# Fewer input buffers, more output buffers, and eleven of 64 transposes moved to VectorE in a matmul with rotary embedding

## The chip, the cores and the metric

The kernel runs on one core of a Trainium2 chip. The metric is the time of one execution in device microseconds (us), measured on the chip; lower is better. A profile is one such execution with its trace. The span in a profile is some 1.75 us shorter than the time of the same execution (168.5 against 170.29 us for the profiled run of the kernel before).

## The reference

The kernel multiplies x by a weight matrix and rotates each head of the product by position.

```python
# x: (16, 512, 768), weight: (768, 768), cos and sin: (512, 64), 12 heads of 64
y = np.matmul(x, weight).reshape(batch, seq, n_heads, head_dim)
y1, y2 = y[..., :32], y[..., 32:]
out1 = y1 * cos1 - y2 * sin1      # cos1, sin1: first halves, by position
out2 = y2 * cos2 + y1 * sin2
out = np.concatenate([out1, out2], axis=-1)
```

Inputs and outputs are fp32. The kernel multiplies in fp16 and accumulates in fp32.

## The kernel before

The 8,192 rows of x make 64 tiles of 128 rows. Two tiles are a pair, numbered n = 0 to 31. A tile is loaded (SyncE's queue), cast to fp16 (ScalarE, `xc`), transposed by six TensorE instructions into PSUM (`pt`), copied to SBUF (ScalarE, `xT`) and multiplied by the weights (12 matmuls into `psy`). VectorE multiplies a whole pair by cosine and sine at once ("rope", `tq`), GpSimd adds the two products (`ov`), and a DMA issued on ScalarE's queue stores the pair.

```python
AHEAD = 8
AHEAD_B = 4
ALONE = 3                      # the last three pairs are done tile by tile
...
def by_blocks(n, s):
    return False               # no tile goes through transpose_blocks
...
xpool = ctx.enter_context(tc.tile_pool(name="xpool", bufs=24))   # x, fp32
opool = ctx.enter_context(tc.tile_pool(name="opool", bufs=4))    # output pairs
...
def load_blocks(n):
    if n >= NP or not by_blocks(n, 1):
        return
    ...
    src = x[b].rearrange("(j a r) (q k) -> r q a j k", r=SB, a=R, q=NQ)
    dst = xss[n, 1].rearrange("p (j k) -> p j k", j=NQ)
    for q in (0, 2, 1, 3):
        eng = nc.sync if q < 2 else nc.scalar
        eng.dma_start(out=dst[ts(q, R)], in_=src[r, q])
...
def transpose_blocks(n, s):    # 32x32 blocks, as four-byte words
    ...
    nc.vector.transpose(out=..., in_=x16.pop((n, s)).bitcast(FP32))
...
for n in range(2, NP):
    while loaded < min(NP, n + AHEAD):
        load_plain(loaded)
        loaded += 1
    if n + 1 < NP and by_blocks(n + 1, 1):
        transpose_blocks(n + 1, 1)
    for s in (0, 1):
        for c in CHUNKS:
            mm(n, s, *c)
        upto("turn", 2 * n + s + 3)     # TensorE transposes and ScalarE copies
        upto("cast", 2 * n + s + 5)     # ScalarE casts
        ...
    if n >= 3:
        store(n - 3, nc.scalar)
    load_blocks(n + AHEAD_B)
    if n < NP - ALONE:
        rope_pair(n)                    # VectorE, then the add on GpSimd
```

Block loads and block transposes are thus written already, and switched off. ScalarE works through its casts, its copies and its DMA issues strictly in order. A DMA issue that has to wait holds everything after it (in the runs below a copy on ScalarE stood for 2.35 us behind a block load's issue and for 5.14 us behind a store's).

Of the kernel before, what the change touches and what calls it, by code (L numbers as in the profile page):

```python
# [12 lines left out]
MULT = mybir.AluOpType.mult  # L13
ADD = mybir.AluOpType.add
# [3 lines left out]
def kernel(  # L18
# [9 lines left out]
    nc = tc.nc  # L28
    P = nc.NUM_PARTITIONS

    B, S, H = x.shape
    NH = int(n_heads)
    D = H // NH
    HD = D // 2
# [3 lines left out]
    SB = S // P  # L38
    NP = B * SB // 2
    CHUNKS = [(t, e) for t in range(NT) for e in range(2)]  # L40
    AHEAD = 8
    AHEAD_B = 4
    ALONE = 3

# [3 lines left out]
    def where(n, s):  # L48
        return 2 * (n // SB) + s, n % SB

    def by_blocks(n, s):
        return False

    konst = ctx.enter_context(tc.tile_pool(name="konst", bufs=1))
    ident = konst.tile([P, P], FP16)
# [2 lines left out]
    csn = konst.tile([P, 2, SB, D], FP32)  # L58
    w_raw = konst.tile([P, NT, 2, H], FP32)
    w_sb = konst.tile([P, NT, 2, H], FP16)  # L60

    xpool = ctx.enter_context(tc.tile_pool(name="xpool", bufs=24))
    bpool = ctx.enter_context(tc.tile_pool(name="bpool", bufs=AHEAD_B + 1))
    cpool = ctx.enter_context(tc.tile_pool(name="cpool", bufs=6))
    tpool = ctx.enter_context(tc.tile_pool(name="tpool", bufs=9))
    rpool = ctx.enter_context(tc.tile_pool(name="rpool", bufs=3))
    opool = ctx.enter_context(tc.tile_pool(name="opool", bufs=4))
    pt_pool = ctx.enter_context(tc.tile_pool(name="pt", bufs=2, space=bass.MemoryType.PSUM))
    py_pool = ctx.enter_context(tc.tile_pool(name="py", bufs=2, space=bass.MemoryType.PSUM))
    cold_ps = pt_pool.tile([P, 512], FP32, tag="pt", name="cold_ps")  # L70
# [1 line left out]
    xss, x16, xTT, psys, tqs, ovs = {}, {}, {}, {}, {}, {}  # L72
# [7 lines left out]
    def load(n, s):  # L80
        b, r = where(n, s)
        xss[n, s] = xpool.tile([P, H], FP32, tag="xs", name="xs")
        nc.sync.dma_start(  # L83
            out=xss[n, s], in_=x[b].rearrange("(p r) h -> r p h", r=SB)[r]
        )

    def load_plain(n):
        for s in (0, 1):
            if n < NP and not by_blocks(n, s):
                load(n, s)  # L90
# [40 lines left out]
    def transpose_blocks(n, s):  # L131
        xT = tpool.tile([P, NT, P, 2], FP16, tag="xT", name="xT")
        nc.vector.transpose(
            out=xT.bitcast(FP32).rearrange("p t m e -> p (t m e)"),
            in_=x16.pop((n, s)).bitcast(FP32),
        )
        xTT[n, s] = xT.rearrange("p t m e -> p t e m")
# [5 lines left out]
    def psum(n, s):  # L143
        if n < NP - ALONE:
            if n not in psys:
                psys[n] = py_pool.tile([P, 3, 512], FP32, tag="psy", name="psy")
                if n < 2:
                    nc.tensor.matmul(  # L148
                        psys[n][:, 1], cold[:, 0:P], cold, start=True, stop=False
                    )  # L150
            cut = 512 if s == 0 else 256
            return [
                (psys[n][:, s, ds(s * 256, cut)], 0, cut, n < 2 and s == 1),
                (psys[n][:, s + 1, 0 : H - cut], cut, H, n < 2 and s == 0),
            ]
        if (n, s) not in psys:
            if (2 * (n - NP + ALONE) + s) % 3 == 1:
                psys[n, s] = [
                    pt_pool.tile([P, 512], FP32, tag="pt", name="psz") for _ in (0, 1)
                ]  # L160
            else:
                ps = py_pool.tile([P, 3, 512], FP32, tag="psy", name="psy")
                psys[n, s] = [ps[:, 0], ps[:, 1]]
        lo, hi = psys[n, s]
        return [(lo, 0, 512, False), (hi[:, 0 : H - 512], 512, H, False)]

    def mm(n, s, t, e):
        for ps, lo, hi, joined in psum(n, s):
            nc.tensor.matmul(  # L169
                ps,  # L170
                xTT[n, s][:, t, e, :],
                w_sb[:, t, e, lo:hi],
                start=((t, e) == CHUNKS[0] and not joined),
                stop=((t, e) == CHUNKS[-1] and not (joined and s == 0)),
            )

    def rope(n, c0, c1, ps):
        r = n % SB
        nh = (c1 - c0) // D
        if n not in tqs:  # L180
            tqs[n] = rpool.tile([P, 2, 2 * H], FP32, tag="tq", name="tq")
            ovs[n] = opool.tile([P, 2 * H], FP32, tag="ov", name="ov")
        nc.vector.tensor_tensor(  # L183
            out=tqs[n][:, :, c0:c1].rearrange("p j (h d) -> p j h d", d=D),
            in0=ps.rearrange("p (h d) -> p h d", d=D)
            .unsqueeze(1).broadcast_to((P, 2, nh, D)),
            in1=csn[:, :, r, :].unsqueeze(2).broadcast_to((P, 2, nh, D)),
            op=MULT,
        )

    def add(n, c0, c1, eng):
        w = c1 - c0
        tq = tqs[n][:, :, ds(c0, w)]
        eng.tensor_tensor(  # L194
            out=ovs[n][:, ds(c0, w)].rearrange("p (h t d) -> p h t d", t=2, d=HD),
            in0=tq[:, 0].rearrange("p (h t d) -> p h t d", t=2, d=HD),
            in1=tq[:, 1].rearrange("p (h t d) -> p h t d", t=2, d=HD)[:, :, ::-1, :],
            op=ADD,
        )

    def rope_pair(n):
        rope(n, 0, 2 * H, psys[n].rearrange("p b n -> p (b n)"))
        add(n, 0, 2 * H, nc.gpsimd)

    def rope_alone(n, s):
        for ps, lo, hi, _ in psum(n, s):
            rope(n, s * H + lo, s * H + hi, ps)



    def rope_last(n, s, engs):
        r = n % SB
        for (ps, lo, hi, _), eng in zip(psum(n, s), engs):
            nh = (hi - lo) // D
            q = tqs[n][:, 1, ds(s * H + lo, hi - lo)]
            ph = ps.rearrange("p (h d) -> p h d", d=D)
            for o, j in ((q.rearrange("p (h d) -> p h d", d=D), 1), (ph, 0)):
                nc.vector.tensor_tensor(  # L218
                    out=o, in0=ph, op=MULT,
                    in1=csn[:, j, r, :].unsqueeze(1).broadcast_to((P, nh, D)),  # L220
                )
            nc.vector.tensor_tensor(  # L222
                out=ovs[n][:, ds(s * H + lo, hi - lo)].rearrange(
                    "p (h t d) -> p h t d", t=2, d=HD
                ),
                in0=ps.rearrange("p (h t d) -> p h t d", t=2, d=HD),
                in1=q.rearrange("p (h t d) -> p h t d", t=2, d=HD)[:, :, ::-1, :],
                op=ADD,
            )
            store(n, eng, s * H + lo, s * H + hi)  # L230

    def store(n, eng, c0=0, c1=2 * H):
        b, r = where(n, 0)
        dst = out.rearrange("b (p r) h -> r p b h", r=SB)[r, :, b : b + 2]
        src = ovs[n].rearrange("p (b h) -> p b h", b=2)
        if c1 - c0 < 2 * H:
            s = c0 // H
            dst = dst[:, s, c0 - s * H : c1 - s * H]
            src = src[:, s, c0 - s * H : c1 - s * H]
        eng.dma_start(out=dst, in_=src)  # L240
# [15 lines left out]
    nc.sync.dma_start(out=sin_sb, in_=sin.rearrange("(p r) d -> p r d", r=SB))  # L256
    for n in range(2, AHEAD):
        load_plain(n)
# [5 lines left out]
    def upto(what, k):  # L264
        k += min(4, max(0, k - 41) // 4)
        while done[what] < min(k, 2 * NP):
            n, s = divmod(done[what], 2)
            done[what] += 1
            if what == "cast":
                cast(n, s, nc.scalar)  # L270
            elif not by_blocks(n, s):
                transpose(n, s, nc.scalar)
# [13 lines left out]
    for k, c in enumerate(CHUNKS):  # L286
# [8 lines left out]
        out=csn[:, 1, :, HD:D], in0=sin_sb[:, :, 0:HD], scalar1=-1.0  # L295
    )
    rope_pair(0)
    upto("cast", 6)
    mm(1, 0, *CHUNKS[-1])
# [4 lines left out]
    upto("turn", 6)  # L304
    upto("cast", 8)
    rope_pair(1)

    loaded = AHEAD
    for n in range(2, NP):

        while loaded < min(NP, n + AHEAD):
            load_plain(loaded)
            loaded += 1
        if n + 1 < NP and by_blocks(n + 1, 1):
            transpose_blocks(n + 1, 1)
        for s in (0, 1):
            for c in CHUNKS:
                mm(n, s, *c)
            upto("turn", 2 * n + s + 3)
            upto("cast", 2 * n + s + 5)  # L320
            if n >= NP - ALONE:
                if (n, s) != (NP - 1, 1):
                    rope_alone(n, s)
                    add(n, s * H, (s + 1) * H, nc.gpsimd)
        if n >= 3:
            store(n - 3, nc.scalar)
        load_blocks(n + AHEAD_B)
        if n < NP - ALONE:
            rope_pair(n)
    store(NP - 3, nc.scalar)  # L330
    store(NP - 2, nc.scalar)
    store(NP - 1, nc.scalar, 0, H)
    rope_last(NP - 1, 1, (nc.sync, nc.sync))


# [33 lines left out]
```

## Time and profile before

| | kernel before |
|---|---|
| time, three runs | 169.1 us median (168.88 to 169.13) |
| time of the profiled run | 170.29 us (span 168.5) |
| TensorE busy | 154.7 us, 92% |
| VectorE, ScalarE, GpSimd busy | 69%, 59%, 65% |
| largest stall of TensorE after the start | 2.50 us at 55.7 us |

The profile cuts the span into 40 slices, in which a digit is the busy share in tenths. Groups of waits give who waited, for whom, the total us, how often, and the longest. The lines are in the prediction. "Granted clock" is the share of TensorE's full clock that the chip granted in a stretch.

### The profile page before, as it was taken

Reading aid. Unit: us, or ns where it says so; the run is one execution under the profiler, and the core shown is the slowest. Engines: PE = TensorE matmul, PEld = TensorE weight load, DVE = VectorE, ACT = ScalarE, POOL = GpSimd, SP = SyncE. Lnnn points to the kernel's source line nnn. Section 1 sums busy time; section 2 is a strip of 40 time slices with the busy share of each in tenths; the row PEclk is TensorE's granted clock in tenths of the full one; section 3 lists DMA queues with packets and bytes.
Section 4 is the critical chain, followed back from the end, with each engine's and each line's share of the span. In section 5 each row is a group of like instructions: output and inputs, shape, how many; then the busy total and the mean of one; then the engine's idle time right before and its main releaser. Section 6 shows DMA issues by size and latency. Waiting matters only on the chain.

```text
span 168.5 us, 2869 instructions
## 1 busy us (share of the span) xinstructions
PE 154.7 (92%) x1170; PEld 99.1 (59%) x1170; DVE 116.0 (69%) x58; ACT 99.6 (59%) x125; POOL 109.4 (65%) x38
## 2 busy tenths in 40 slices
PE   7799999999999499999999999999999999999900
PEld 2455666666666256666666666676666766665500
DVE  0566976777777707777777777776767676789970
ACT  3523876666773356677666677787898788610000
POOL 0000597739952945749997777777876767679980
PEclk9999999999999969999999999999999999999995
DMA  4999999999999999999999997444433444458666
GB/s 168 365 399 402 398 402 402 405 411 322 416 373 412 411 417 415 411 414 414 415 420 405 397 330 292 191 187 160 157 123 153 164 187 189 187 222 339 256 251 243
DMA packets 19390, 53.18 MB, mean 316 GB/s; under 512 B 1840, under 2 KB 2224, under 8 KB 19376
## 3 DMA queue, kind: packets, MB, share of 16 engines
q1 hardware_dynamic: 10656, 28.19, 43.3%
q10 hardware_dynamic: 8720, 24.81, 37.8%
q8 instruction: 9, 0.15, 0.3%
q14 instruction: 5, 0.04, 0.1%
HBM read 27.82 MB, written 25.17 MB: 314 GB/s over the span
## 4 chain that ended last, share of the span: by engine, by line
PE 66%; DMA 17%; DVE 6%; POOL 3%; ACT 1%; issue 1%; POOLq 1%; SPq 1%; ACTq 0%; DVEq 0%
PE psy L169 55%; PE pt L126 10%; DMA xs<-in_x_dram 7%; DVE tq L183 6%; DMA out_dram<-ov 6%; DMA w_raw<-in_weight_dram 4%; POOL ov L194 3%; POOLq L364 1%; SPq L83 1%; ACT xT L76 1%; ACT xc L76 1%; ACTq L240 0%; POOLq L194 0%; DVEq L183 0%
## 5 line engine op out<-in xcount | busy, mean ns | idle before, releaser
L194 POOL TENSOR_TENSOR ov<-tq 128x1536 f32<-128x1536 f32 (+1 forms) x34 | 109.2, 3220 | 54.1 <-DVE tq L183 36.4
L169 PE MATMUL psy<-w_sb,xT 128*128 128x512 f16 (+1 forms) x744 | 132.3, 328 | 2.6 <-ACT xT L76 2.5
L183 DVE TENSOR_TENSOR tq<-psy,csn 128x3072 f32<-128x3072 f32 (+2 forms) x35 | 102.6, 2945 | 39.2 <-PE psy L169 37.8
L169 PEld LDWEIGHTS <-xT 128*128 128x128 f16 x768 | 73.2, 98 | 46.2 <-ACT xT L76 2.7
L76 ACT COPY xT<-pt 128x768 f16<-128x768 f16 x62 | 49.2, 800 | 40.0 <-PE pt L126 35.4
L76 ACT CAST xc<-xs 128x768 f16<-128x768 f32 x62 | 55.4, 901 | 8.3 <-DMA xs<-in_x_dram 8.2
L126 PEld LDWEIGHTS <-xc 128*128 128x128 f16 x384 | 26.5, 99 | 10.9 <-ACT xc L76 1.9
L126 PE MATMUL pt<-ident,xc 128*128 128x128 f16 x384 | 31.6, 220 | 1.4 <-ACT xT L76 0.5
L244 PE MATMUL cold_ps<-cold 128*128 128x512 f16 x16 | 5.6, 494 | 1.2 <-DVE cold L249 1.2
L110 DVE CAST w_sb<-w_raw 128x768 f16<-128x768 f32 x6 | 3.4, 560 | 2.1 <-DMA w_raw<-in_weight_dram 2.1
L169 PE MATMUL psz<-w_sb,xT 128*128 128x512 f16 (+1 forms) x24 | 4.2, 326 | 0.0
L78 DVE CAST xc<-xs 128x768 f16<-128x768 f32 x2 | 1.9, 948 | 3.1 <-DMA xs<-in_x_dram 3.1
L244 PEld LDWEIGHTS <-cold 128*128 128x128 f16 x16 | 1.8, 123 | 3.3 <-issue 1.9
L183 DVE TENSOR_TENSOR tq<-psz,csn 128x1024 f32<-128x1024 f32 (+1 forms) x4 | 3.6, 948 | 0.0
L78 DVE COPY xT<-pt 128x768 f16<-128x768 f16 x2 | 1.1, 558 | 1.7 <-PE pt L126 1.7
L76 ACT ACT_TABLE_LOAD x1 | 1.3, 1283 | 1.1 <-PEq L350 1.1
L222 DVE TENSOR_TENSOR ov<-psy,tq 128x512 f32<-128x512 f32 (+1 forms) x2 | 1.1, 557 | 0.1
L218 DVE TENSOR_TENSOR psy<-psy,csn 128x512 f32<-128x512 f32 (+1 forms) x2 | 1.1, 556 | 0.0
L218 DVE TENSOR_TENSOR tq<-psy,csn 128x512 f32<-128x512 f32 (+1 forms) x2 | 1.1, 554 | 0.0
L249 DVE MEMSET cold<- 128x256 uint32 x1 | 0.3, 272 | 0.9 <-PEq L350 0.9
L148 PE MATMUL psy<-cold 128*128 128x512 f16 x2 | 0.8, 379 | 0.0
L293 DVE COPY csn<-sin_sb 128x128 f32<-128x128 f32 x1 | 0.2, 226 | 0.2 <-DMA sin_sb<-in_sin_dram 0.2
(6 smaller groups left out, 0.8 us busy)
## 6 DMA issues: line engine op xcount, KB each, us to landing
xs<-in_x_dram SPq DMA_DIRECT2D x64, 384.0 KB, 8.4
out_dram<-ov ACTq DMA_DIRECT2D x31, 768.0 KB, 5.6
w_raw<-in_weight_dram SPq DMA_DIRECT2D x6, 384.0 KB, 7.4
out_dram<-ov ACTq DMA_DIRECT2D x1, 384.0 KB, 3.6
out_dram<-ov SPq DMA_DIRECT2D x1, 256.0 KB, 2.3
csn<-in_cos_dram SPq DMA_DIRECT2D x1, 128.0 KB, 7.9
sin_sb<-in_sin_dram SPq DMA_DIRECT2D x1, 128.0 KB, 6.5
out_dram<-ov SPq DMA_DIRECT2D x1, 128.0 KB, 3.4
```

The costliest lines, as they stand in the source:

```text
L76: eng.copy(out=o, in_=i_)
L78: eng.tensor_copy(out=o, in_=i_)
L83: nc.sync.dma_start(out=xss[n, s], in_=x[b].rearrange("(p r) h -> r p h", r=SB)[r])
L110: nc.vector.tensor_copy(out=w_sb[:, t, e], in_=w_raw[:, t, e])
L126: nc.tensor.transpose(pt[:, t, e, :], xc[:, t, e, :], ident)
L169: nc.tensor.matmul(ps, xTT[n, s][:, t, e, :], w_sb[:, t, e, lo:hi], start=((t, e) == CHUNKS[0] and not joined), stop=((t, e) == CHUNKS[-1] ...
L183: nc.vector.tensor_tensor(out=tqs[n][:, :, c0:c1].rearrange("p j (h d) -> p j h d", d=D), in0=ps.rearrange("p (h d) -> p h d", d=D) .unsqu ...
L194: eng.tensor_tensor(out=ovs[n][:, ds(c0, w)].rearrange("p (h t d) -> p h t d", t=2, d=HD), in0=tq[:, 0].rearrange("p (h t d) -> p h t d", ...
L218: nc.vector.tensor_tensor(out=o, in0=ph, op=MULT, in1=csn[:, j, r, :].unsqueeze(1).broadcast_to((P, nh, D)),)
L222: nc.vector.tensor_tensor(out=ovs[n][:, ds(s * H + lo, hi - lo)].rearrange("p (h t d) -> p h t d", t=2, d=HD), in0=ps.rearrange("p (h t d) ...
L244: nc.tensor.matmul(cold_ps, cold[:, 0:P], cold, start=True, stop=True)
L364: with _tile.TileContext(nc) as tc:
```

## The change

The intent is to stop the loads from running far ahead of the work (ten input buffers instead of 24), to give the stores more slack (six output buffers instead of four), to take 66 transposes off TensorE, and to shorten the end.

```diff
-    AHEAD = 8
+    AHEAD = 7
     def by_blocks(n, s):
-        return False
+        return s == 1 and n % 2 == 1 and 6 < n < NP - ALONE
-    xpool = ctx.enter_context(tc.tile_pool(name="xpool", bufs=24))
+    xpool = ctx.enter_context(tc.tile_pool(name="xpool", bufs=10))
-    opool = ctx.enter_context(tc.tile_pool(name="opool", bufs=4))
+    opool = ctx.enter_context(tc.tile_pool(name="opool", bufs=6))
-    def rope_pair(n):
-        rope(n, 0, 2 * H, psys[n].rearrange("p b n -> p (b n)"))
-        add(n, 0, 2 * H, nc.gpsimd)
+    def rope_pair(n, step=2 * H):
+        ps = psys[n].rearrange("p b n -> p (b n)")
+        for c in range(0, 2 * H, step):
+            rope(n, c, c + step, ps[:, ds(c, step)])
+            add(n, c, c + step, nc.gpsimd)
     # cut: rope_last now ropes the last 256 columns first and has GpSimd add them,
     # does the first 512 in place on VectorE, and stores the two parts on two queues
-        while loaded < min(NP, n + AHEAD):
-            load_plain(loaded)
-            loaded += 1
+        load_plain(n + AHEAD - 2)
-            rope_pair(n)
+            rope_pair(n, 2 * H if n < NP - ALONE - 1 else H)
```

More of the change, by code (lines that the diff above doesn't have):

```diff
@@ L207, in rope_alone, with rope_last @@
             rope(n, s * H + lo, s * H + hi, ps)
-    def rope_last(n, s, engs):
-        r = n % SB
-        for (ps, lo, hi, _), eng in zip(psum(n, s), engs):
-            nh = (hi - lo) // D
-            q = tqs[n][:, 1, ds(s * H + lo, hi - lo)]
-            ph = ps.rearrange("p (h d) -> p h d", d=D)
-            for o, j in ((q.rearrange("p (h d) -> p h d", d=D), 1), (ph, 0)):
-                nc.vector.tensor_tensor(
-                    out=o, in0=ph, op=MULT,
-                    in1=csn[:, j, r, :].unsqueeze(1).broadcast_to((P, nh, D)),
-                )
-            nc.vector.tensor_tensor(
-                out=ovs[n][:, ds(s * H + lo, hi - lo)].rearrange(
-                    "p (h t d) -> p h t d", t=2, d=HD
-                ),
-                in0=ps.rearrange("p (h t d) -> p h t d", t=2, d=HD),
-                in1=q.rearrange("p (h t d) -> p h t d", t=2, d=HD)[:, :, ::-1, :],
-                op=ADD,
-            )
-            store(n, eng, s * H + lo, s * H + hi)
+    def rope_last(n, s):
+        (ps, _, cut, _), (pz, _, _, _) = psum(n, s)
+        c0, c1, c2 = s * H, s * H + cut, (s + 1) * H
+        rope(n, c1, c2, pz)
+        add(n, c1, c2, nc.gpsimd)
+        nh = cut // D
+        q = tqs[n][:, 1, c0:c1]
+        ph = ps.rearrange("p (h d) -> p h d", d=D)
+        for o, j in ((q.rearrange("p (h d) -> p h d", d=D), 1), (ph, 0)):
+            nc.vector.tensor_tensor(
+                out=o, in0=ph, op=MULT,
+                in1=csn[:, j, n % SB, :].unsqueeze(1).broadcast_to((P, nh, D)),
+            )
+        nc.vector.tensor_tensor(
+            out=ovs[n][:, c0:c1].rearrange("p (h t d) -> p h t d", t=2, d=HD),
+            in0=ps.rearrange("p (h t d) -> p h t d", t=2, d=HD),
+            in1=q.rearrange("p (h t d) -> p h t d", t=2, d=HD)[:, :, ::-1, :],
+            op=ADD,
+        )
+        store(n, nc.sync, c0, c1)
+        store(n, nc.scalar, c1, c2)
     def store(n, eng, c0=0, c1=2 * H):
@@ L306 @@
     rope_pair(1)
-    loaded = AHEAD
     for n in range(2, NP):
-        while loaded < min(NP, n + AHEAD):
-            load_plain(loaded)
-            loaded += 1
+        load_plain(n + AHEAD - 2)
         if n + 1 < NP and by_blocks(n + 1, 1):
@@ L332 @@
     store(NP - 1, nc.scalar, 0, H)
-    rope_last(NP - 1, 1, (nc.sync, nc.sync))
+    rope_last(NP - 1, 1)
 _INS = ['x', 'weight', 'cos', 'sin', 'n_heads']
```

## The prediction

> **What bounds the kernel now.** I read the page's list of busy engines first, then the busy tenths, then the chain of work that ended last. TensorE is the candidate: it is busy 92% of the span and every other engine at most 69%.
>
> ```profile
> span 168.5 us, 2869 instructions
> PE 154.7 (92%) x1170; PEld 99.1 (59%) x1170; DVE 116.0 (69%) x58; ACT 99.6 (59%) x125; POOL 109.4 (65%) x38
> PE   7799999999999499999999999999999999999900
> DMA  4999999999999999999999997444433444458666
> ```
>
> A busy TensorE alone proves little, so the reader should look at the zeros, the 4 in the fifteenth slice (59 to 63 us), and the last row: the DMA engines are full until slice 24 (about 100 us) and then less than half busy. The chain says whether TensorE really sets the pace. Its columns are start, length and what ran:
>
> ```profile
> 58.25 3.40 PE psy L169 x12
> 61.65 0.64 PE pt L126 x6
> 62.29 2.04 PE psy L169 x12
> 64.33 0.34 PE pt L126 x6
> 64.67 1.95 PE psy L169 x12
> 66.62 0.33 PE pt L126 x6
> 66.95 1.95 PE psy L169 x12
> ```
>
> From 16.4 us to 37.5 us and from 58 us to 148 us it is nothing but TensorE: 12 matmuls of 1.95 us, then six transposes of 0.34 us, per tile of 128 rows: 2.285 us a tile, 4.57 us a pair. The first line is the exception. The groups of waits say why:
>
> ```profile
> DVE tq L183 <- PE psy L169: 37.8, 27, 5.6
> POOL ov L194 <- DMA out_dram<-ov: 17.7, 10, 5.1
> ACT xT L76 <- POOL ov L194: 4.6, 1, 4.6
> PE psy L169 <- ACT xT L76: 2.5, 1, 2.5
> ```
>
> Columns: total us, times, longest. Lines two to four are one sequence, and the timeline from 44 to 62 us gives its order. GpSimd's add for a pair waits 5.14 us for one of four output buffers, because that buffer's store takes 9.63 us to land; ScalarE, which issues stores in order between its copies, then sits 4.58 us on a store whose add isn't done; TensorE, needing the xT that ScalarE has not copied, idles 2.50 us at 55.7 us. The table of windows shows the aftermath (the columns here are stretch, its length, busy time of PE, PEld, DVE, ACT, POOL, then granted clock, DMA share, GB/s):
>
> ```profile
> 37.00:57.00 20.00, 18.75 (x151) 12.37 (x149) 14.91 (x5) 11.14 (x14) 13.50 (x4) 1.00 1.02 386
> 57.00:62.00 5.00, 3.75 (x18) 2.11 (x19) 1.88 (x1) 3.09 (x4) 3.74 (x2) 0.69 1.03 414
> 62.00:92.00 30.00, 30.00 (x238) 19.86 (x237) 20.29 (x7) 20.72 (x26) 21.80 (x7) 0.99 1.03 414
> ```
>
> The granted clock falls to 0.69, so 12 matmuls take 3.40 instead of 1.95 us. Whole cost: matmul groups start at 53.30 and 64.67 us, three tiles later; 11.37 us instead of 3 x 2.285 = 6.86, so **4.5 us are lost to one stall**.
>
> The end is a second regime. TensorE stops at 159.96 us (timeline), the profile at 168.5. There GpSimd is the last link: its adds run back to back from 151.47 to 163.77 us (one of 3.46, five of about 1.77), and the store of the last one closes the span.
>
> **What the Trainium skill says.** "VectorE: DVE Perf Modes", The three transpose paths: VectorE transposes only within blocks of 32x32, and puts 128x128 bf16 at 311 ns. That is why the change needs a special load, which puts the blocks where a block-wise transpose yields the whole one. The trace before has no such instruction. "TensorE: Matmul & The Clock Gate", What's actually happening: an idle TensorE is throttled to half rate and needs about 3.4 us of activity to be released. The trace agrees in kind: 0.69 mean clock in the 5 us after an idle 2.50 us. "DMA: Bandwidth & Descriptors", Why small descriptors are slow: about 3 cycles of overhead per packet on 32-byte beats. The block loads move rows of 768 B, the plain ones 3,072 B: (24+3)/24 = 1.125 against (96+3)/96 = 1.03, an estimate of 9% more DMA time for those tiles. No row of the trace isolates it. "SBUF — State Buffer", Who interferes with whom: a VectorE instruction with one SBUF input, outside the two-port modes, doesn't hold up GpSimd; it lists copy, cast and tensor_scalar as ops that enter those modes, not the transpose. So I charge GpSimd nothing; the trace can't confirm it yet.
>
> **The change, part by part.**
>
> 1. *Ten input buffers instead of 24, six output buffers instead of four.* With 24 buffers the loads run far ahead and hold the DMA engines at 386 to 414 GB/s until 92 us, and in that time stores take 8.2 to 8.7 us (median by window) against 3.6 us afterwards. An add for pair n needs the buffer of pair n-4, whose store is issued one iteration earlier: some 8 us, against up to 9.6. With six buffers it is pair n-6, stored three iterations earlier: about 8 + 2 x 4.57 = 17 us. Even the slowest store of the old trace fits. I take the whole stall away: **-4.5 us**.
>
> 2. *Eleven tiles (second tile of pairs 7, 9, ... 27) no longer transposed on TensorE.* 11 x 6 = 66 transposes go, each group 0.336 us on the chain: 11 x 0.336 = **-3.7 us**, all on the path, since TensorE sets the pace there. The weight loads from the interleaved xT should cost nothing more: weight loads from the equally interleaved xc take 99 ns and those from a contiguous xT 98 ns. Off the path ScalarE loses 11 copies of 0.80 us. VectorE gains 11 transposes of 384 four-byte words. Its own instructions of 256 and 512 words took 0.42 and 0.69 us, so about 0.55 us each, an estimate. VectorE has 1.21 us idle per pair before each rope; a pair shrinks to 4.57 - 0.17 = 4.40 us on average, and with 0.28 us of transpose per pair some 0.76 us stay idle. Cost on the path: 0.
>
> 3. *Block loads.* Four DMAs of 96 KB for a tile instead of one of 384 KB, two of them issued by ScalarE's queue (0.38 us a store's issue in the trace, beside running copies). Demand in steady state: 1.573 MB per pair read and written, over 4.40 us, is 357 GB/s; the old trace sustained 414 with both directions. 9% on a sixth of the loads leaves the DMA engines near 88% of that rate. Hidden, but without much room.
>
> 4. *The end.* Pair 28 is roped and added in halves, so GpSimd starts its tail after half a rope (1.7 instead of 3.4 us) and ends each later add about 1.6 us sooner: the add of the 63rd tile near 162.2 us on the old clock of events rather than 163.8. The last tile now does its 256 columns first, by VectorE (0.68 us) and a GpSimd add, then 512 columns in three VectorE passes of 0.62 us, so VectorE ends at about 162.6 instead of 163.15, and three stores end on two queues. They then land together, so I credit **-1.3 us**, not 1.6.
>
> Sum: 169.1 - 4.5 - 3.7 - 1.3 = 159.6. I add 0.4 us for small waits that a fuller interleaving of short loads, stores and casts usually leaves (my choice): **160.0 us**.
>
> **The rivals.**
>
> *DMA becomes the bound.* For it: all 53.2 MB must now move evenly, at 357 GB/s and with shorter rows, where prefetch used to put the reads early. Against it: 414 GB/s over 30 us in the window table. If short rows cut the rate to 340, the 145 us from first load to last would have to become 156, and the time some 164 to 167 us.
>
> *The stall moves to ScalarE's queue.* Its store and block-load issues wait in order, and a block load is issued only four pairs ahead, while the shifting schedule of casts closes that distance late: the cast for pair 27 comes about one tile step after its load was issued. With landings of 5 to 8 us ScalarE may wait 3 to 5 us there. For it: just such a ScalarE wait of 4.58 us caused the old stall. Against it: by then copies are three tiles ahead, nearly 7 us of work for TensorE. If TensorE does stop once, with the slower clock after, it costs about what was gained: 164 us.
>
> *The stall was hiding nothing and only half of it goes*: stores still slow while the first buffers fill (up to about 35 us the gate does not hold anything back). Then 162 us.
>
> *VectorE or GpSimd as new bound.* VectorE needs 3.36 + 0.28, GpSimd 3.46 of 4.40 us per pair; both have room, so I give this little.
>
> **Range and chances.** All three gains act on a chain that I could follow, and they are separate, so the centre is 160.0. If parts 1 and 2 land in full and the end brings 2 us or more, 158; if a stall returns somewhere or DMA presses, 163.5. For less than 2% (above 165.7) both a new stall and half of the transposes' gain would have to go wrong: 6%, slower 1%, faster 93%.
>
> **What would show it.** Right: no slice of TensorE below 9 between 20 us and the end; granted clock 1.0 throughout; in the waits, GpSimd on stores well below 17.7 us and no wait of TensorE on ScalarE over 0.5 us; TensorE's matmul groups 1.95 us with gaps of nothing after the eleven tiles; block transposes near 0.55 us; DMA rate flat near 350 GB/s rather than 414 then 165; TensorE's end 8.2 us sooner (near 152) and the tail after it about 7.2 instead of 8.5 us. Wrong: TensorE waiting on ScalarE with a DMA behind it, a VectorE transpose waiting for a cast and delaying the rope behind it, or transposes of over 1 us.

## The result, and the profile after

The changed kernel took **164.21 us** (median of four runs, 162.74 to 165.36); the kernel before took 169.12 us (four runs, 168.88 to 170.31). The ratio of the two is 0.9667, 95% interval 0.9584 to 0.9751. Such a ratio, here and below, is the mean time of one kernel's runs over that of the other's in the same rounds, so it isn't quite the ratio of the medians. Executions over 1.5% slower than the fastest of the same kernel are left out of the means. The direction was right and the gain, some 5 us, was a little over half of the 9 us forecast. The median lies 0.7 us above the stated range; the ratio applied to 169.1 us gives 163.5, its upper edge.

The page of the changed kernel, profiled in a run of 164.27 us:

```profile
span 162.5 us, 2775 instructions
PE 150.2 (92%) x1104; PEld 94.4 (58%) x1104; DVE 120.8 (74%) x68; ACT 91.2 (56%) x114; POOL 110.2 (68%) x40
PE   7799999999998999999999999999989899999910
PEclk9999999999999999999999999999999999999995
DMA  4999999999999999999999999999997545459766
```

The hole in TensorE's row has gone and the clock (PEclk) no longer dips. Three 8s have come instead, and the DMA engines stay full until slice 30 instead of 24. Groups of waits of the changed kernel (some rows left out):

```profile
POOL ov L194 <- DVE tq L183: 47.1, 26, 18.5
ACT xc L76 <- DMA xb<-in_x_dram: 6.7, 3, 3.0
ACT xT L76 <- DMA xs<-in_x_dram: 5.6, 3, 2.4
PE pt L126 <- ACT xc L76: 1.6, 3, 0.8
PE psy L169 <- ACT xT L76: 0.8, 2, 0.6
```

GpSimd no longer waits for stores at all. But ScalarE now waits for DMAs, the loads of blocks (`xb`) among them, and TensorE waits for ScalarE. TensorE's timeline gives the four places (start, length, instruction, and in brackets the idle time just before, with what ended it):

```profile
51.37 2.12 PE L169 MATMUL psy<-w_sb,xT 128*128 128x512 f16 x12 [0.61 <-ACT xT L76]
60.50 2.12 PE L169 MATMUL psy<-w_sb,xT 128*128 128x512 f16 x12 [0.16 <-ACT xT L76]
120.82 0.51 PE L126 MATMUL pt<-ident,xc 128*128 128x128 f16 x6 [0.46 <-ACT xc L76]
128.61 0.51 PE L126 MATMUL pt<-ident,xc 128*128 128x128 f16 x6 [0.76 <-ACT xc L76]
```

Because ends of matmuls are modelled, I take the loss at each place from the starts instead: group before, plus 1.95 us per 12 matmuls, against the start here. That is 0.77, 0.32, 0.62 and 0.92 us, **2.6 us** in all. ScalarE's timeline ahead of the first place:

```profile
47.03 0.41 ACTq L243 DMA_DIRECT2D out_dram<-ov  x1
47.25 0.90 ACT L76 CAST xc<-xb 128x768 f16<-128x768 f32 x1
47.46 3.01 ACTq L102 DMA_DIRECT2D xb<-in_x_dram  x2
50.51 0.80 ACT L76 COPY xT<-pt 128x768 f16<-128x768 f16 x1 [2.35 <-DMA xs<-in_x_dram]
```

ACTq is ScalarE's instruction queue. Between 47.46 and 50.47 us it stands at two block-load issues, the second of which goes out at 50.12 us, just after an x load that SyncE had issued at 42.55 us landed, at 50.10 us. Only then may the copy run that TensorE needs. The later two places look different: at 117.69 us ScalarE's cast of a block tile had waited 3.01 us for the block load itself.

### The profile page after: what moved, and what is told of

Its sections match the earlier page's. It is cut to its first block, busy times and chain, and to the rows that moved or that the text cites. A ratio compares the mean times of both kernels' runs of the same rounds, so it can differ in the third digit from the quotient of the medians.

```text
span 162.5 us, 2775 instructions
## 1 busy us (share of the span) xinstructions
PE 150.2 (92%) x1104; PEld 94.4 (58%) x1104; DVE 120.8 (74%) x68; ACT 91.2 (56%) x114; POOL 110.2 (68%) x40
## 4 chain that ended last, share of the span: by engine, by line
PE 51%; DMA 27%; DVE 7%; ACT 6%; issue 2%; ACTq 2%; SPq 1%; POOLq 1%; POOL 1%; DVEq 0%
PE psy L169 43%; DMA xs<-in_x_dram 13%; DMA xb<-in_x_dram 10%; PE pt L126 7%; DVE tq L183 7%; DMA w_raw<-in_weight_dram 4%; ACT xc L76 4%; ACT xT L76 2%; ACTq L243 1%; SPq L83 1%; POOLq L363 1%; POOL ov L194 1%; ACTq L102 0%; ACTq L76 0%; POOLq L194 0%
## 5 line engine op out<-in xcount | busy, mean ns | idle before, releaser
L194 POOL TENSOR_TENSOR ov<-tq 128x1536 f32<-128x1536 f32 (+2 forms) x36 | 110.0, 3067 | 47.9 <-DVE tq L183 47.1
L169 PE MATMUL psy<-w_sb,xT 128*128 128x512 f16 (+1 forms) x744 | 129.7, 326 | 0.8 <-ACT xT L76 0.8
L183 DVE TENSOR_TENSOR tq<-psy,csn 128x3072 f32<-128x3072 f32 (+3 forms) x37 | 103.4, 2807 | 28.7 <-PE psy L169 28.7
L76 ACT COPY xT<-pt 128x768 f16<-128x768 f16 x51 | 40.5, 800 | 36.7 <-PE pt L126 29.2
L76 ACT CAST xc<-xs 128x768 f16<-128x768 f32 x51 | 44.8, 904 | 9.1 <-DMA xs<-in_x_dram 8.1
L126 PE MATMUL pt<-ident,xc 128*128 128x128 f16 x318 | 26.0, 219 | 2.6 <-ACT xc L76 1.6
L126 PEld LDWEIGHTS <-xc 128*128 128x128 f16 x318 | 21.6, 98 | 11.0 <-ACT xc L76 3.6
L76 ACT CAST xc<-xb 128x768 f16<-128x768 f32 x11 | 10.0, 905 | 5.8 <-DMA xb<-in_x_dram 5.8
L133 DVE STREAM_TRANSPOSE xT<-xc 128x384 f32<-128x384 f32 x11 | 6.2, 568 | 0.0
L226 DVE TENSOR_TENSOR ov<-psy,tq 128x512 f32<-128x512 f32 x1 | 0.7, 691 | 0.0
```

The source lines that it names most:

```text
L76: eng.copy(out=o, in_=i_)
L126: nc.tensor.transpose(pt[:, t, e, :], xc[:, t, e, :], ident)
L133: nc.vector.transpose(out=xT.bitcast(FP32).rearrange("p t m e -> p (t m e)"), in_=x16.pop((n, s)).bitcast(FP32),)
L169: nc.tensor.matmul(ps, xTT[n, s][:, t, e, :], w_sb[:, t, e, lo:hi], start=((t, e) == CHUNKS[0] and not joined), stop=((t, e) == CHUNKS[-1] ...
L183: nc.vector.tensor_tensor(out=tqs[n][:, :, c0:c1].rearrange("p j (h d) -> p j h d", d=D), in0=ps.rearrange("p (h d) -> p h d", d=D) .unsqu ...
L194: eng.tensor_tensor(out=ovs[n][:, ds(c0, w)].rearrange("p (h t d) -> p h t d", t=2, d=HD), in0=tq[:, 0].rearrange("p (h t d) -> p h t d", ...
```

## The experiments

All kernels below gave correct results. Each has four timed executions; the median and spread are given. The runs come from three rounds on three chips, each with its own executions of the kernel before, and the changed kernel was timed in an earlier round only. Differences between two experiments of under 1 us rest on medians and traces alone.

### Which buffers removed the old stall?

`e_out6` is the kernel before with six output buffers; `e_gate` is the kernel before with ten input buffers ("the gate": a load has to wait until one of the ten is free); `e_gate_out6` has both.

```diff
-    opool = ... bufs=4        # e_out6, e_gate_out6
+    opool = ... bufs=6
-    xpool = ... bufs=24       # e_gate, e_gate_out6
+    xpool = ... bufs=10
```

> The kernel before with six output buffers instead of four, all else as before (24 input buffers, no block transposes, old end). Theory A, that the stall at 55 us is an add waiting for an output buffer: six buffers alone remove it, 4.5 us, so about 164.6 us, no granted clock below 0.98 in the middle, and GpSimd waits on stores near 0 instead of 17.7 us, while the DMA engines stay full until about 92 us. Theory B, that the flood of loads is the cause and only the gate helps: 168 to 169 us, with the stall only moved to a later pair.

> The kernel before with ten input buffers instead of 24, all else as before (four output buffers). Theory A: after about 38 us the loads no longer fill the DMA engines (rate near 345 GB/s), stores land in 4 to 6 us rather than 8 to 9.6, so the GpSimd waits shrink from 17.7 to under 8 us and the stall is mostly gone: 165 to 167 us. Theory B (the flood is the whole cause): 164.6 us.

> Part 1 of the change alone: ten input and six output buffers, no block transposes, the old end. Predicted worth 4.5 us: 164.6 us, no idle TensorE over 0.3 us after 17 us. If the new waits of ScalarE in the changed kernel came from the gate and not from the block loads, they would be here as well, with TensorE idle for 1 to 3 us and 166 us.

| run | median us (spread) | ratio (95%) |
|---|---|---|
| e_out6 | 169.16 (168.90 to 170.73) | 0.9969 (0.9853 to 1.0085) |
| e_gate | 166.12 (165.88 to 166.46) | 0.9761 (0.9685 to 0.9838) |
| e_gate_out6 | 166.10 (165.88 to 166.16) | 0.9756 (0.9682 to 0.9830) |

My theory A fell. With six output buffers the stall is still there, 3.07 us of idle TensorE; with ten input buffers it is gone, and six output buffers then add nothing. The waits of `e_out6` say how that can be:

```profile
POOL ov L194 <- DVE tq L183: 52.8, 28, 18.2
ACT xT L76 <- POOL ov L194: 5.1, 1, 5.1
PE psy L169 <- ACT xT L76: 3.1, 1, 3.1
```

GpSimd doesn't wait for a store once, so no add was late, and still ScalarE stands for 5.1 us. The second line names GpSimd, but the add of the pair being stored had ended long before; where a named engine had long been done, it was another wait of the same instruction. The compiled program shows which one. In it every DMA of SyncE's and ScalarE's queues reports to one of eight completion counters (DMAHW0 to 7), taken in turn, and an issue waits until the counter's previous DMA has landed. ScalarE's first stores in the kernel before (a store needs its counter, DMAHW, and its add, Pool):

```
21 L240 DMACopy out_dram<-ov 128x2x768 [waits DMAHW5_49,Pool_49]
26 L240 DMACopy out_dram<-ov 128x2x768 [waits DMAHW2_49,Pool_49]
31 L240 DMACopy out_dram<-ov 128x2x768 [waits DMAHW7_49,Pool_49]
36 L240 DMACopy out_dram<-ov 128x2x768 [waits DMAHW5_49,Pool_49]
41 L240 DMACopy out_dram<-ov 128x2x768 [waits DMAHW2_49,Pool_49]
46 L240 DMACopy out_dram<-ov 128x2x768 [waits DMAHW0_49,Pool_49]
```

Over these six stores the counter advances by five or six from store to store, so four or five x loads lie between two stores. Counting eight DMAs back from the sixth store, the store of pair 5, gives the 36th x tile, the second of pair 17. In the trace SyncE issued that load at 45.87 us; by the counter's own events it landed at 56.90 us, and the sixth store went out at 56.98 us:

```profile
51.91 0.90 ACT L76 CAST xc<-xs 128x768 f16<-128x768 f32 x1
56.98 0.38 ACTq L240 DMA_DIRECT2D out_dram<-ov  x1
57.40 0.80 ACT L76 COPY xT<-pt 128x768 f16<-128x768 f16 x1 [4.58 <-POOL ov L194]
```

The match is no single case. The packed trace keeps the counters' events, and in it seven of the first ten stores of the kernel before went out 0.07 to 0.08 us after the landing that their counter waited for; in `e_out6` the same load landed at 57.15 us and the sixth store went out at 57.23 us. With ten input buffers the counter advances by three in the steady state: in `e_gate` the sixth store went out at 51.19 us, and the load eight DMAs back, issued at 39.04 us, had landed at 43.97 us, 7 us before it.

### Is it ScalarE's queue that makes the stall?

`e_store_pool` leaves the flood of loads and moves the stores inside the loop to GpSimd's queue.

```diff
-            store(n - 3, nc.scalar)
+            store(n - 3, nc.gpsimd)
```

> The kernel before, its 29 stores inside the loop issued from GpSimd's queue instead of ScalarE's; 24 input buffers and four output buffers stay, so the flood of loads stays. Theory C: the old stall is ScalarE's store issue waiting for a DMA completion counter that an x load far ahead still holds (the store issued at 56.98 us; the load issued at 45.87 us landed 11.1 us later, at 56.97); off ScalarE's queue it no longer stops the copies: the TensorE gap at 55 us goes, 166 us, unless GpSimd's own adds, held now behind the stores, run out of time, which would bring a later gap by VectorE waiting for GpSimd, 166 to 170 us. Theory B (stores are slow to land, adds wait): the gap stays, 169 to 170.7 us.

It took 178.82 us (178.60 to 179.80; ratio 1.0534, 1.0447 to 1.0620), so my total was wrong. The part that it was run for came out: TensorE's first gap after the start is at 80 us.

```profile
37.00:57.00 20.00, 20.00 (x160) 13.18 (x158) 14.98 (x5) 13.99 (x18) 13.69 (x7) 1.00 1.02 412
80.17 2.11 PE L169 MATMUL psy<-w_sb,xT 128*128 128x512 f16 x12 [1.60 <-DVE tq L183]
89.92 2.11 PE L169 MATMUL psy<-w_sb,xT 128*128 128x512 f16 x12 [0.44 <-DVE tq L183]
```

The first line is of the table of windows, in the prediction's columns: from 37 to 57 us TensorE never stopped although the DMA engines moved 412 GB/s, nor did it to 62 us. So the old stall was a store held on ScalarE's queue, and the loads alone don't make it. The new loss is that GpSimd spends 0.72 us on each issue, waited 19.2 us in total for stores, and ended late. This run, `e_out6` and the matches of times above leave Theory C without a rival that I can see. A run that changes the counters alone was not made, since the framework assigns them.

### What did the block transposes bring?

`e_no_blocks` is the changed kernel with all tiles transposed on TensorE again.

```diff
-        return s == 1 and n % 2 == 1 and 6 < n < NP - ALONE
+        return False
```

> The changed kernel with the block transposes taken away: buffers, gate and the new end stay, all 64 tiles are transposed by TensorE. Theory: against the run with part 1 alone the new end is worth about 0.9 us (7.64 us instead of 8.54 from TensorE's last matmul to the end), so 163.7 us; and the changed kernel (164.2) gains nothing from its eleven saved transposes, because the 3 us that TensorE waits on ScalarE eat the 3.7 us. Rival: the waits come from the gate, then this one has them too and takes 167 us, 3.7 us over the changed kernel.

It took 165.53 us (165.43 to 165.57; ratio 0.9724, 0.9651 to 0.9798) and TensorE has no gap after 17 us. Against `e_gate_out6` the new end is worth 0.6 us in the medians (0.9 in the traces, counted from the start of TensorE's last matmul group: 9.78 against 10.66 us); `AHEAD` changed with it. Against the changed kernel the blocks bring only 1.3 us (165.53 to 164.21) where 3.7 us was forecast. The two medians are of different rounds, and the changed kernel's own runs spread over 2.6 us; with the mean of its three fast runs, 163.7 us, it is 1.8 us. So the new waits come with the blocks, and the gate alone does not make them. The rival that I gave for this run, 167 us, is out.

### Short rows, narrow DMAs, or the queue that issues them?

`e_rows768` loads the eleven tiles in rows of 768 B without the block shape. `e_4x32` loads them by four DMAs of 32 partitions with full rows. Both keep TensorE's transposes. `e_4x32_act` then issues two of each four from ScalarE's queue.

```diff
 # e_rows768: tile padded to [P, 4, 200], so that a row of 3,072 B becomes four of 768 B
+    nc.sync.dma_start(out=xss[n, s][:, :, 0:192], in_=src.rearrange("p (j k) -> p j k", j=4))
 # e_4x32
+    for q in (0, 2, 1, 3):
+        nc.sync.dma_start(out=xss[n, s][ts(q, R)], in_=src[ts(q, R)])
 # e_4x32_act, on top of it
+        eng = nc.sync if q < 2 else nc.scalar
```

> The changed kernel without block transposes, but its eleven tiles come in rows of 768 B (one DMA of 128 partitions into a padded tile), so only the row size differs from the run without blocks (165.5 us). Theory 1, short rows are what fills the DMA engines: in the changed kernel the two big queues took 91.5% of 162.5 us on 16 engines for 53.0 MB against 81% of 168.5 us before, 12 us more for 4.3 MB in short rows, so they cost twice the time per byte instead of my 9%; then this run has a DMA time 10 to 12 us above the run without blocks, and about the same total, 165.5 to 166 us. Rival: it is the 32-partition shape, and this run has the DMA time of the run without blocks.

> The changed kernel without block transposes, its eleven tiles loaded by four DMAs of 32 partitions with full rows of 3,072 B, all from the SyncE queue. Theory 1 (row size): DMA time as in the run without blocks, within 2 us; total 165.5 to 166. Rival, 32 partitions per DMA reach only part of the engines' ports: 10 to 12 us more DMA time. Theory 2, that nine DMAs per two pairs on the eight completion counters make the queues wait for each other: total 166.5 or more, with ScalarE's copies waiting on DMAs after 35 us.

> The run with four DMAs of 32 partitions and full rows (165.0 us, no gap of TensorE), with two of each four issued from ScalarE's queue instead of SyncE's. It puts the suspected cause back without short rows, block transposes or fewer TensorE transposes. If loads on ScalarE's in-order queue are what costs, TensorE's gaps come back: 1 to 3 us in all, 166 to 168 us, with ScalarE's copies held behind an issue that waits for a DMA. If it stays at 165.0 us, the cost belongs to the block loads themselves.

The DMA time is the two large queues' share of the span, added and multiplied by the span.

| run | DMA time us | median us (spread) | ratio (95%) |
|---|---|---|---|
| e_no_blocks | 144.1 | 165.53 (165.43 to 165.57) | 0.9724 (0.9651 to 0.9798) |
| e_rows768 | 146.1 | 165.19 (164.90 to 165.30) | 0.9684 (0.9641 to 0.9727) |
| e_4x32 | 145.9 | 165.02 (164.64 to 165.36) | 0.9676 (0.9631 to 0.9721) |
| e_4x32_act | not used | 165.59 (165.42 to 165.99) | 0.9740 (0.9676 to 0.9804) |
| changed kernel | 148.7 | 164.21 (162.74 to 165.36) | 0.9667 (0.9584 to 0.9751) |

Theory 1 in the strong form, twice the time per byte, fell: 768 B rows cost 2.0 us more DMA time, and nothing in the total. The eleven tiles are 4.3 MB, which at 144.1 us for 53.0 MB are 11.8 us, so short rows would cost about 17% more, not 100%. This DMA time isn't work alone, though: `e_4x32`, with full rows, has 1.8 us more than `e_no_blocks` too. The packets themselves, which the trace keeps, say it better: in `e_rows768` the median packet of 768 B took 36 ns and that of 3,072 B 121 ns, and 4 x 36 is 19% more than 121. Narrow DMAs and the higher number of DMAs cost nothing in the total either. The extra DMA time of the changed kernel was in part packets waiting, and not work: its short packets have the same median of 36 ns, but took 15.3 us of the 16 engines together, against 13.1 us in `e_rows768`.

`e_4x32_act` did bring ScalarE's waits and TensorE's gaps back, at 42.14 and 70.11 us, but small: 0.28 and 0.37 us idle, 0.6 us in the total where I had said 1 to 3. The direction is as the theory says, and the size isn't. Its ScalarE issues stand at another place in the loop, with data wanted later; that this is the reason was not tested.

### Block loads off ScalarE's queue, and block loads earlier

`e_sync` issues all four block loads from SyncE's queue. `e_ahead5` leaves the queues and issues the block loads five pairs ahead.

```diff
-            eng = nc.sync if q < 2 else nc.scalar      # e_sync
+            eng = nc.sync
-    AHEAD_B = 4                                        # e_ahead5
+    AHEAD_B = 5
```

> The changed kernel with all four block loads issued from SyncE's queue, none from ScalarE's. Theory 2 says that 4 to 6 us of ScalarE's waits are block loads that hold its in-order queue until a completion counter is free (one issue took 3.01 us at 47 us): without them TensorE keeps 1 to 1.5 us of its 2.6 us of gaps, 163.0 us. Theory 1 (the DMA engines are simply full): no change, 164.2 us, as the data come no earlier.

> The changed kernel with block loads issued five pairs ahead instead of four (six block buffers). Theory 3, the shifted casts near the end outrun the block loads (ScalarE waited 3.01 us at 114.7 us and 2.8 us at 123.4 us, followed by TensorE gaps of 0.6 and 0.9 us): these two gaps go, 1.5 us, 162.7 us; the gaps near 50 and 60 us stay. If the DMA engines are full, the gaps only move: 164.2 us.

`e_sync` took **161.34 us** (161.17 to 161.75; ratio 0.9466, 0.9414 to 0.9517). It is better than both kernels. Its interval doesn't meet that of the changed kernel, nor do the times (at most 161.75 against at least 162.74 us), and `e_ahead5`, which keeps ScalarE's issues, took 164.51 us in the same rounds. Its page and its table of windows (stretch, length, busy PE, PEld, DVE, ACT, POOL, granted clock, DMA share, GB/s):

```profile
span 159.6 us, 2796 instructions
PE   7899999999999999999999999999999999999900
...
62.00:92.00 30.00, 30.00 (x226) 19.36 (x224) 24.31 (x11) 19.55 (x25) 23.52 (x7) 1.00 1.04 386
```

The same stretch of the changed kernel:

```profile
62.00:92.00 30.00, 30.00 (x229) 19.53 (x228) 23.98 (x11) 18.72 (x25) 22.92 (x8) 1.00 1.04 369
```

TensorE has no gap. The same bytes in the same short rows now move at 386 GB/s, against 369 GB/s; so the DMA engines were not the bound there. Against `e_no_blocks` the blocks now bring 4.2 us, and against `e_4x32`, of the same rounds, 3.7 us, which is the forecast. I had expected 163.0 us and underestimated the effect: it removes both kinds of gap. ScalarE is no longer held by the issues, and the loads no longer start late because ScalarE came late to them: no cast of a block tile waits for its load here.

`e_ahead5` took 164.51 us (164.21 to 165.89; ratio 0.9663, 0.9604 to 0.9721). The late gaps at 120 and 128 us went, as theory 3 said, but the early ones, at 42.72 and 49.16 us now instead of 51 and 60, grew to 0.90 and 1.69 us, and the total stayed. Loading earlier does not help while ScalarE's queue is the one that waits.

### Six output buffers, and more blocks

`e_sync_out4` is `e_sync` with four output buffers; `e_sync_all` is `e_sync` with 22 block tiles, one in every pair from 7 to 28.

```diff
-    opool = ... bufs=6                                               # e_sync_out4
+    opool = ... bufs=4
-        return s == 1 and n % 2 == 1 and 6 < n < NP - ALONE          # e_sync_all
+        return s == 1 and 6 < n < NP - ALONE
```

> The changed kernel with all block loads on SyncE's queue (161.3 us) and four output buffers instead of six. With the gate alone GpSimd waited 2.3 us on stores, once, and nothing was lost; here the DMA engines are fuller (386 GB/s, stores land in 6.9 us at the median), and the add has about 8 us: GpSimd waits 5 to 15 us in all, still hidden, 161.3 to 161.8 us. If six buffers are needed, 163 us or more with a TensorE gap.

> The changed kernel with block loads on SyncE's queue and the second tile of every pair from 7 to 28 transposed by VectorE (22 tiles instead of 11). TensorE loses another 11 x 0.336 = 3.7 us: 157.6 us if nothing else binds. VectorE has 3.36 + 0.57 of 4.24 us per pair, and the DMA engines need 371 GB/s: if they are the next bound (386 GB/s was the most seen with short rows), there are gaps of TensorE on loads and 159 to 163 us.

`e_sync_out4` took 161.53 us (161.33 to 161.74; ratio 0.9498, 0.9436 to 0.9560), with GpSimd waiting 3.5 us on stores, hidden. The two extra output buffers bring nothing measurable. `e_sync_all` took 170.87 us (169.08 to 174.75, two of its four runs slow; ratio 0.9966, 0.9863 to 1.0069), worse than I allowed for. ScalarE waits for block loads:

```profile
ACT xc L76 <- DMA xb<-in_x_dram: 26.3, 12, 4.1
```

TensorE stops six times, for up to 2.21 us, and the rate from 92 to 122 us is only 302 GB/s. So it isn't the 386 GB/s limit that I had in mind. SyncE's own waits say what holds the loads (L102 is the issue of a block load):

```profile
SPq L102 <- DMA out_dram<-ov: 31.6, 17, 3.5
```

The landings match again: block loads go out at 99.20, 109.42, 119.12 and 127.76 us, 0.01 to 0.06 us after the landing of the store that had held their counter. From 60 to 130 us such waits for stores come to 22.4 us, and waits for a cast to free a block buffer to 1.1 us. So by the trace it is the eight counters, in SyncE's ordered queue: with six DMAs a pair, the DMA eight places back is little more than one pair old. Two of TensorE's stops also brought a halved clock (the last section).

## Why the prediction was right or wrong

**That TensorE sets the pace, and that the gains add:** right. In `e_sync`, where nothing new stalls, TensorE's last group ends at 151.9 us against the forecast "near 152", and the span is 159.6 us.

**"4.5 us are lost to one stall":** two errors. The cause was wrong: it was no add waiting for one of four output buffers but a store issue waiting on ScalarE's queue (theory C); the GpSimd wait that I read first happened in the same microseconds. The gate removes it for another reason than I gave, so that the stall went in full was in part luck; the output buffers, half of the argument, did nothing. And **the size was taken from one run and subtracted from others**. The profiled run of 170.29 us had the stall and a clock of 0.69 after it; the three timed runs behind 169.1 us can't have had the clock loss in full. The kernel before falls into two groups: runs of 168.7 to 169.4 us (mean granted clock 0.981 to 0.987 where it is listed) and of 170.2 to 171.3 us (0.970 to 0.981). The profile of `e_out6` has the stall without the dip, 12 matmuls in 2.12 us and not 3.40. (One line of the profile I also misread: the 4 in TensorE's row is its fourteenth slice, 54.8 to 59.0 us, not the fifteenth.) So the stall is worth about 3.0 us against 169.1 (169.1 to 166.1) and 4.2 us in spans against the profiled run (168.5 to 164.3). Against 169.1 this term was 1.5 us too large. Against the slower group it was right: of the 26 runs of the kernel before 18 are in it, with a median of 170.7 us, 4.6 us above the gate's.

**"-3.7 us, all on the path":** right as a term, 3.7 to 4.2 us in `e_sync`. In the changed kernel it was eaten, in part, by the second rival, "the stall moves to ScalarE's queue": 1.3 us was left, so 2.4 us were lost. I had named the late casts (they are the gaps at 120 and 128 us) and had trusted three tiles of lead to hide the waits. I had not seen the early gaps, in which an issue itself stands. The sign that I had named for being wrong, TensorE waiting on ScalarE with a DMA behind it, was there. That this rival's figure, 164 us, is the measured one is partly chance: it meant one stop with a slower clock, and four short stops without one came, beside a mis-sized stall. The details of the term held: a block transpose took 0.568 us (0.55 estimated), weight loads from `xT` still 98 ns, a GpSimd add of a pair 3.46 us as before.

**"-1.3 us" for the end:** 0.6 us in the medians, 0.9 in the traces. It was 0.4 to 0.7 us too large.

**Block loads hidden, "9% more DMA time":** hidden they are in the total once ScalarE doesn't issue them; a short row's measured cost is about 19% by packets (17% by DMA time). The rival that DMA becomes the bound is out for eleven tiles.

**The sum:** 1.5 (stall) + 2.4 (blocks) + 0.7 (end) - 0.4 (my allowance) = 4.2 us, which is 164.2 - 160.0. By median the whole gain of 4.9 us is 3.0 from the gate, 0.6 from the end and 1.3 from the blocks. These medians are of different rounds, and the first number depends on which group of runs one starts from.

## What to carry to other kernels

Issue DMAs that may have to wait from a queue whose engine has nothing else to do: here two of four small loads on ScalarE's queue cost 2.9 us of 164.2 by medians, and the transfers themselves nothing. That has its limit where the DMAs are many: with 22 block tiles SyncE's queue waited 31.6 us for the counters of stores, and the kernel took 170.87 us. When a wait names an engine that had long been done, look in the compiled program for the other things that the instruction waits for. And before a loss seen in a profile is subtracted from a median, compare the time of the profiled run with the timed ones: a clock dip that only some runs have is not in all of them.

## What the Trainium skill lacked or had wrong

- "Trainium Kernel Development and Optimization", Key Constraints: it says that issuing DMAs from several engines only saves the sequencer's issue time. It lacks the cost on the other side: an issue that waits held ScalarE's copies for up to 2.35 us (block loads, changed kernel) and 5.1 us (stores, `e_out6`), and the choice of queue moved this kernel from 164.2 to 161.3 us. No page that I read tells of issues that wait for a completion counter's previous DMA.
- "TensorE: Matmul & The Clock Gate", What's actually happening: it has an idle window of about 3.4 us throttle the clock, and the window free-running. The traces agree on the grid: the clock steps that they hold are 3.41 us, or multiples of it, apart. But the window need not be idle throughout. The clock was halved for one window after windows with 2.50 us (kernel before), 2.03 and 2.21 us (`e_sync_all`) of idle TensorE, and stayed full in `e_out6`, where a boundary cuts the stop of 3.07 us into 1.22 and 1.84 us. Nor does the page say that one short stop can split a kernel's times into two groups. The two of the kernel before are 1.7 us apart, which is what 3.41 us at half clock costs (an estimate; one trace of the slower group is kept and none of the faster). The kernel before, by windows:

```profile
55.52:58.93 3.41, 0.91 (x10) 0.48 (x7) 3.36 (x1) 1.53 (x3) 3.23 (x2) 1.00 1.04 416
58.93:62.34 3.41, 3.41 (x18) 1.96 (x16) 0.00 (x0) 1.56 (x4) 1.99 (x1) 0.50 1.04 416
```

- "VectorE: DVE Perf Modes", The three transpose paths: this section has 311 ns for 128x128 bf16 only. A transpose of 128x384 four-byte words took 568 ns here, and GpSimd's adds beside it kept their 3.46 us.
- "DMA: Bandwidth & Descriptors", Why small descriptors are slow: its 3 cycles a packet give 9% for rows of 768 B against 3,072 B; the packets show 19% (36 and 121 ns). A straight line through these two has a fixed cost of 7.7 ns a packet, an estimate.
